# Attention scores of one token tile as three products of hi and lo parts instead of one float32 product, in a fused two-layer trunk

## The chip, the cores and the metric

The kernel runs on one core of a Trainium2 chip. The metric is device time in microseconds for one launch. The engines are called PE (TensorE, matrix products; its weight loads are listed as PEld), DVE (VectorE), ACT (ScalarE), POOL (GpSimd) and SP (SyncE, which here only issues DMA transfers). Each engine works through its own instructions in the order in which they were written for it.

## The reference, cut to what matters

Two layers, each a half-step SwiGLU feed-forward, a mixer and a second half-step feed-forward, with layer norms between. The input has 256 tokens of 1024 features in float32. The part of the mixer that the change touches:

```python
q = _rope(q.reshape(bsz, seq, N_DIFF_HEADS, 2, DIFF_HEAD_DIM), cos, sin)   # 8 heads, 2 maps of 64
k = _rope(k.reshape(bsz, seq, N_DIFF_HEADS, 2, DIFF_HEAD_DIM), cos, sin)
s = jnp.einsum('bqhmd,bkhmd->bhmqk', q_blk, k).astype(jnp.float32) * scale
s = jnp.where(mask, s, neg)                      # causal
p = jax.nn.softmax(s, axis=-1)
a = p[:, :, 0] - lam * p[:, :, 1]
return jnp.einsum('bhqk,bkhe->bqhe', a.astype(v.dtype), v)
```

## The kernel before, in words

The 256 tokens are two tiles of 128; t=0 is the first, t=1 the second. In causal attention the first tile's queries see 128 keys and the second tile's see 256.

**Weights and the split.** All weights are streamed once, 1 MB at a time, by the SP queue into a `raw` buffer (L153; 4 buffers). A float32 product is made of products in the faster float32r format: ACT writes a rounded copy `whi` (L166), DVE the remainder `wlo = raw - whi` (L168). There are 8 buffers for hi and 8 for lo parts. Activations are kept as hi and lo in the same way.

**The projections.** `gemm_a2` (L210 to L237) computes one 256-wide block of an input projection, features on partitions: per chunk eight products with `whi` on 512 columns (L220: the hi and lo parts of x side by side), later eight with `wlo` on 256 columns (L227). Then ACT evacuates half of the bank into `r` (L228, the instruction is kept as `emptied[0]`) and DVE adds the other half into `z` (L230 or L232, kept as `added[0]`). `gemm_b` and `rows_b` (L208) compute the other products with tokens on partitions. Products go to 4 "main" PSUM banks; scores, transposes and attention outputs to 4 "side" banks.

**The mixer.** After the values come four head pairs, hp0 to hp3 (L680 to L683). For each, `rope` (L563 to L581) projects and rotates q, then k: four small DMAs on the SP queue exchange the halves (L569), DVE multiplies by the cosine (L572), POOL by the sine (L573), DVE adds (L577). Then `attend` (L583 to L678) is set beside the stream of projections: scores (L597; the 64 features of one map lie on 64 partitions, so the two maps, m = 0 and 1, use two row groups), mask and maximum on DVE (L609), exp with sum on ACT (L611), the difference of the two maps (L620), transposes on PE (L634, L639), which ACT copies out as `aT` (L636 for t=1, 128x512; L641 for t=0, 128x256), the product with the values (L647, L649), RMS norm (L652 to L666, with POOL), transposes (L671) and the split result `hb` (L676, L677). After hp3 come the gates, whose projections end in `gz` (DVE) and L693 (ACT).

**Order.** PE's order is written by hand: a clock counts the weight of projections done (`beat`, 0.65 for a hi part and 0.35 for a lo part), and a generator that was set `beside` goes on when its delay has passed; `yield d` in it asks for the next turn d later. The order of DVE, ACT, POOL and SP is made by a scheduler that follows priorities; `behind(x)` asks for a place behind instruction x. What an engine finds at the head of its queue it waits for, whatever stands behind it.

**The filler.** After the last products, `idle` (L271 to L291) issues 52 products whose result nobody reads: 10 of 128x128, 16 of 64x256 and 16 of 64x128 on two row groups, 2 of 128x512 and 8 of 128x64, all in float32r, into two side banks.

Of the kernel before, what the change touches and what calls it, by code (L numbers as in the profile page):

```python
# [11 lines left out]
F32 = mybir.dt.float32  # L12
F32R = mybir.dt.float32r
BF16 = mybir.dt.bfloat16
I32 = mybir.dt.int32
AF = mybir.ActivationFunctionType
ALU = mybir.AluOpType
AX = mybir.AxisListType

P = 128  # L20
D = 1024
T = 256
# [7 lines left out]
HD = 64  # L30
# [20 lines left out]
def trunk(ctx, tc, x, xT, w13a, w13b, w2, wb, wqk, wa, wbr, wo, gateb, sgug, sgub, sguwT, sgubias, lam, diffg,  # L51
          lng, lnb, lngT, lnbT, cosT, sinT, out):
    nc = tc.nc
    V, A, G, PE = nc.vector, nc.scalar, nc.gpsimd, nc.tensor
# [15 lines left out]
    def name(s):  # L70
        serial[0] += 1
        return f"{s}_{serial[0]}"

    def bank():
        return psum.tile([P, 512], F32, tag="main", name=name("bank"))

    def side_bank():
        return psum.tile([P, 512], F32, tag="side", name=name("sbank"))

    def slots(s, n, dtype=F32):  # L80

        return [act.tile([P, 512], dtype, tag="slot", name=name(s)) for _ in range((n + 1) // 2)]
# [8 lines left out]
    def parts(f):  # L91
        return (lambda k: f(k)[:, :T]), (lambda k: f(k)[:, T:])
# [40 lines left out]
    def beside(task, delay):  # L133
        tasks.append([clock[0] + delay, task])
# [6 lines left out]
    latest, added, emptied, silu, turned_by = [None, None], [None], [None], [None], [None]  # L141

    def behind(ins):

        return tc.issue_after(ins) if ins is not None else nullcontext()

    def stream(src, width=CH, sub=HC, lent=(), after=(None, None)):

        step()
        raw = raw_pool.tile([P, CH], F32, tag="raw", name=name("raw"))
        nc.sync.dma_start(raw[:, :width], src)  # L153
        out = []
        for o in range(0, width, HC):
            if o // HC in lent:
                hi, lo = ([act.tile([P, 512], F32R, tag="slot", name=name(n)) for _ in range(2)] for n in ("lhi", "llo"))
                at = [(hi[j], lo[j]) for j in range(2)]
            else:
                hi = hi_pool.tile([P, HC], F32R, tag="hi", name=name("whi"))  # L160
                lo = lo_pool.tile([P, HC], F32R, tag="lo", name=name("wlo"))
                at = [(hi[:, p : p + sub], lo[:, p : p + sub]) for p in range(0, HC, sub)]
            for p, (h, w) in zip(range(0, HC, sub), at):
                r = raw[:, o + p : o + p + sub]
                with behind(latest[0]):
                    A.activation(h, r, AF.Copy)  # L166
                with behind(after[o // HC] or latest[1]):
                    V.tensor_tensor(out=w, in0=r, in1=h.bitcast(F32), op=ALU.subtract)  # L168
            out.append((hi, lo))
        return out  # L170
# [19 lines left out]
    def rsqrt4(v, scale):  # L190

        ve, y = sm("ve", 4), sm("yi", 4, I32)
        G.tensor_scalar(out=ve, in0=v, scalar1=scale, scalar2=None, op0=ALU.mult)
        G.tensor_scalar(out=y, in0=ve.bitcast(I32), scalar1=-0.5, scalar2=RSQRT_START, op0=ALU.mult, op1=ALU.add)
        y = y.bitcast(F32)
        for e in (-26 / 27, -8 / 9, -2 / 3):
            a, z = sm("nwa", 4), sm("nwy", 4)
            G.tensor_tensor(out=a, in0=y, in1=y, op=ALU.mult)
            G.tensor_tensor(out=a, in0=a, in1=ve, op=ALU.mult)
            G.tensor_scalar(out=a, in0=a, scalar1=3.0 * 2.0 ** e, scalar2=None, op0=ALU.subtract)  # L200
            G.tensor_tensor(out=z, in0=a, in1=y, op=ALU.mult)
            y = z
        return y
# [35 lines left out]
    def rows_b(ps, t, k0, piece, xh, xl, kts, c0=0, n=512):  # L239

        hi, lo = piece
        for j in range(2):
            k, o = k0 + j, j * 512 + c0
            wh, wl = (w[j][:, c0 : c0 + n] if isinstance(w, list) else w[:, o : o + n] for w in (hi, lo))
            three(ps[:, :n], xh(k)[:, t * P : (t + 1) * P], xl(k)[:, t * P : (t + 1) * P], wh, wl,
                  k == 0, k == kts - 1)
        beat(n / 1024)

    def gemm_b(src, kts, xh, xl, done, tail=4, last=()):

        blocks = [[(bank(), c, n) for c, n in (last if t else ()) or ((0, 512),)] for t in range(NT)]
        held = []
        for c in range(0, kts, 4):
            nk = min(4, kts - c)
            for i, piece in enumerate(stream(src[:, c * 512 : (c + nk) * 512], nk * 512)):
                k = c + 2 * i
                if k >= kts - tail:
                    held.append((k, piece))
                    continue
                for t in range(NT):  # L260
                    for ps, o, n in blocks[t]:
                        rows_b(ps, t, k, piece, xh, xl, kts, o, n)
        for t in range(NT):
            for ps, o, n in blocks[t]:
                for k, piece in held:
                    rows_b(ps, t, k, piece, xh, xl, kts, o, n)
                done(t, ps[:, :n], o, n)
        if last:
            idle(held, xh, xl)

    def idle(held, xh, xl):  # L271

        banks = [side_bank() for _ in range(2)]
        (k, (hi, lo)), (k1, (hi1, lo1)) = held[-2:]
        ws = [xh(k)[:, :P], xl(k)[:, :P], xh(k1)[:, :P], xl(k1)[:, :P]]
        ms = [hi[:, :512], lo[:, :512], hi1[:, :512], lo1[:, :512]]

        def one(i, n, m=None):
            r = slice(0, P) if m is None else slice(m * HD, (m + 1) * HD)
            PE.matmul(banks[m or 0][:, :n], ws[i % 4][r], ms[i % 4][r, :n], start=True, stop=True)  # L280

        for i in range(10):
            one(i, P)
        for n in (256, P):
            for i in range(8):
                for m in range(2):
                    one(i, n, m)
        for i in range(2):
            one(i, 512)
        for i in range(8):  # L290
            one(i, 64)  # L291

    def gemm_b2(srcs, xh, xl, done, norm=None):

# [207 lines left out]
    def ffn(l, f, i, norm, last=False):  # L502
# [26 lines left out]
        for j in range(FB, FT, 2):  # L529
            for m, z in gemm_a2([w13a[l, f, j - FB + m] for m in range(2)], both, lambda m: t512("silu")):  # L530
# [4 lines left out]
                if norm is None and j + m == FB:  # L535
                    beside(setup(s[:, :1]), 0)
        ln = Norm(l, i, 2.0 * ALPHA, 4.0 * EPS, s[:, :1], last)
        gemm_b(w2[l, f, 0], FT, hh, hl, lambda t, p, c, n: ln.part(t, 0, p))

        def done(t, p, c, n):  # L540
# [7 lines left out]
    def mixer(l, i, norm):  # L548
        xh, xl = parts(both)
# [33 lines left out]
        def attend(hp, qT, kT):  # L583
# [4 lines left out]
            def rows(z, m, j, o, n):  # L588
                return z[m * HD : (m + 1) * HD, j * T + o : j * T + o + n]

            def scores(t):

                nk = (t + 1) * P
                banks = [side_bank() for _ in range(2)]
                for j in range(2):
                    for m in range(2):
                        PE.matmul(banks[m][:, j * nk : (j + 1) * nk], rows(qT, m, j, t * P, P), rows(kT, m, j, 0, nk),  # L597
                                  start=True, stop=True)
                return banks

            def exps(t, banks):
                nk = (t + 1) * P
                pp = []
                for m in range(2):
                    o = m * 4 + t * 2
                    p = s512("pp", 4)[:, : 2 * nk]
                    for j in range(2):
                        s, a = slice(j * nk, (j + 1) * nk), slice(o + j, o + j + 1)
                        V.tensor_tensor_reduce(out=p[:, s], in0=banks[m][:, s], in1=mask[:, T - nk :], scale=-1.0,  # L609
                                               scalar=BIG, op0=ALU.add, op1=ALU.min, accum_out=mx[:, a])  # L610
                        A.activation(p[:, s], p[:, s], AF.Exp, bias=mx[:, a], scale=-1.0, accum_out=sums[:, a])  # L611
                    pp.append(p)
                return pp

            def less(t, pp):
# [5 lines left out]
                                            in1=pp[0][:, s], op0=ALU.mult, op1=ALU.add)  # L621
                return pp[0]

            banks = [scores(t) for t in (1, 0)]
            second, first = exps(1, banks[0]), exps(0, banks[1])
            V.reciprocal(out=rc, in_=sums[:, 4:])
# [34 lines left out]
            r = rsqrt4(ss, 1.0 / (2 * HD))  # L661
# [18 lines left out]
        for hp in range(HEADS // 2):  # L680
            qT = rope(wqk[l, hp, 0], HD ** -0.5)
            kT = rope(wqk[l, hp, 1], 1.0, hp == HEADS // 2 - 1)
            beside(attend(hp, qT, kT), 4.5)  # L683

        gates = []
        for br, sec in ((0, GA_), (1, GB_)):
# [17 lines left out]
        for t in range(NT):  # L704
            mv = sm("mv", 2)
            V.bn_aggr(out=mv, in_=vst[t])
            r = rsqrt(mv[:, 1:2], EPS)
# [66 lines left out]
    for l in range(DEPTH):  # L774
        norm = ffn(l, 0, 0, norm)
        norm = mixer(l, 1, norm)
        norm = ffn(l, 1, 2, norm, last=l == DEPTH - 1)
# [82 lines left out]
```

## Time and profile before

| what | value |
|---|---|
| median of 3 runs | 1241.08 us (1240.89 to 1241.84) |
| the profiled execution | 1241.04 us |
| its span, first to last instruction | 1239.3 us |
| granted TensorE clock | 1.000 |
| PE busy | 1234.4 us, 100% of the span |
| DVE busy | 874.2 us, 71% |
| ACT busy | 754.7 us, 61% |
| L597, the scores: records in both layers | 128 (64 of 64x256, 64 of 64x128) |

How to read it: a row of the timeline has the start in microseconds from the span's start, the duration, engine, line, operation, output <- input with the names of the program's tiles, shapes, count; in brackets how long the engine had been idle before and what ended that. Consecutive alike instructions are put together in one row (x16). A float32 product leaves two records, a float32r product one. The chain of waits follows the work that ended last back through what released it. In the groups by line the columns behind the count are busy time in all, mean nanoseconds of one, and idle time before.

### The profile page before, as it was taken

To read this page: it belongs to the slowest core of one execution; us is meant where nothing else is said; L and a number is where in the kernel's file an instruction comes from. 1 tells how busy PE (TensorE), PEld (TensorE's weight loads), DVE (VectorE), ACT (ScalarE), POOL (GpSimd) and SP (SyncE) were. 2 spreads that over 40 slices of the span, in tenths; PEclk is the share of its full clock that TensorE was granted. 3 is DMA by queue.
4 is the path that set the end of the run, shared out by engine and by line. 5 is a ranking of instruction groups with operands and counts; after the bars stand their busy time and mean duration, and the time that the engine had idled before them with its cause. 6 is when DMAs were issued, how large, how long until landed. Compare 5 with 4: busy or idle time off the path is not lost.

```text
span 1239.3 us, 17964 instructions
## 1 busy us (share of the span) xinstructions
PE 1234.4 (100%) x6747; PEld 1067.3 (86%) x6747; DVE 874.2 (71%) x1533; ACT 754.7 (61%) x1386; POOL 90.3 (7%) x182
## 2 busy tenths in 40 slices
PE   9999999999999999999999999999999999999998
PEld 8888888888888888888888888888888888888888
DVE  6766567886687977665676765678866879766753
ACT  6776446679665566664466664466885654766640
POOL 0100000244100000000000000003440000000000
PEclk9999999999999999999999999999999999999999
DMA  9765645654743745547545546556456456466540
GB/s 351 279 204 179 229 170 181 231 187 152 266 174 137 257 161 198 185 169 254 196 171 190 190 160 248 204 184 214 172 179 226 149 185 223 170 204 204 173 166 35
DMA packets 40681, 241.89 MB, mean 195 GB/s; under 512 B 5345, under 2 KB 6417, under 8 KB 14481
## 3 DMA queue, kind: packets, MB, share of 16 engines
q1 hardware_dynamic: 36624, 228.08, 52.5%
q0 software_dynamic: 3536, 12.13, 3.0%
q8 instruction: 53, 0.87, 0.3%
q10 hardware_dynamic: 432, 0.52, 0.1%
q14 instruction: 36, 0.29, 0.1%
HBM read 235.47 MB, written 1.05 MB: 191 GB/s over the span
## 4 chain that ended last, share of the span: by engine, by line
PE 97%; ACT 1%; DVE 1%; issue 0%; DMA 0%; SPq 0%; POOL 0%; DVEq 0%; POOLq 0%
PE bank L220 37%; PE bank L208 35%; PE bank L227 19%; PE bank L347 2%; PE sbank L597 1%; PE sbank L483 1%; PE sbank L730 1%; PE sbank L649 1%; ACT pp L611 0%; PE sbank L359 0%; PE sbank L517 0%; PE sbank L647 0%; PE sbank L671 0%; PE sbank L634 0%; DMA swap<-z 0%
## 5 line engine op out<-in xcount | busy, mean ns | idle before, releaser
L168 DVE TENSOR_TENSOR wlo<-raw,whi 128x1024 fp32r<-128x1024 f32 (+1 forms) x442 | 490.0, 1127 | 230.5 <-PE bank L227 127.2
L166 ACT ACTIVATE whi<-raw 128x1024 fp32r<-128x1024 f32 (+1 forms) x442 | 425.9, 978 | 286.5 <-PE bank L220 142.1
L220 PE MATMUL bank<-x,whi 128*128 128x512 f32 x1792 | 425.4, 391 | 0.0
L220 PEld LDWEIGHTS bank<-x,whi 128*128 128x128 f32 x1792 | 330.8, 188 | 66.2
L227 PE MATMUL bank<-x,wlo 128*128 128x256 f32 x1792 | 231.2, 284 | 0.0
L227 PEld LDWEIGHTS bank<-x,wlo 128*128 128x128 f32 x1792 | 225.2, 191 | 5.4
L208 PE MATMUL bank<-whi,hhi 128*128 128x512 f32 (+1 forms) x374 | 141.3, 378 | 0.0
L208 PE MATMUL bank<-wlo,hhi 128*128 128x512 f32 (+1 forms) x374 | 141.0, 377 | 0.0
L208 PE MATMUL bank<-whi,hlo 128*128 128x512 f32 (+1 forms) x374 | 140.9, 377 | 0.0
L228 ACT ACTIVATE r<-bank 128x256 f32<-128x256 f32 x256 | 96.8, 379 | 64.6 <-PE bank L227 64.1
L208 PE MATMUL bank<-whi,x 128*128 128x512 f32 x328 | 106.5, 394 | 0.0
L208 PEld LDWEIGHTS bank<-whi,hhi 128*128 128x128 f32 x374 | 70.4, 188 | 12.9
L208 PEld LDWEIGHTS bank<-whi,hlo 128*128 128x128 f32 x374 | 70.4, 188 | 12.9
L208 PEld LDWEIGHTS bank<-wlo,hhi 128*128 128x128 f32 x374 | 70.4, 188 | 12.7
L208 PEld LDWEIGHTS bank<-whi,x 128*128 128x128 f32 x328 | 61.6, 188 | 12.7
L208 PE MATMUL bank<-wlo,x 128*128 128x512 f32 x164 | 64.0, 390 | 0.0
L407 POOL DMA_DIRECT2D bc<-in_lng x6 | 3.2, 531 | 727.0 <-DVE bc L406 727.0
L489 ACT ACTIVATE xf<-sbank,ln_b,ln_g 128x128 f32<-128x128 f32 x80 | 30.0, 456 | 40.2 <-PE sbank L483 40.2
L230 DVE TENSOR_TENSOR silu<-bank,r 128x256 f32<-128x256 f32 x144 | 54.2, 418 | 0.2
L433 DVE SCALAR_TENSOR_TENSOR xtok<-xtok,bank 128x512 f32<-128x512 f32 (+1 forms) x25 | 16.6, 662 | 42.6 <-PE bank L208 42.6
L573 POOL TENSOR_TENSOR swap<-swap,sin_t 128x512 f32<-128x512 f32 x16 | 28.5, 1780 | 242.4 <-DMA swap<-z 141.9
L208 PE MATMUL bank<-lhi,x 128*128 128x512 f32 x120 | 39.8, 396 | 0.0
(178 smaller groups left out, 1262.1 us busy)
## 6 DMA issues: line engine op xcount, KB each, us to landing
raw<-in_w13a SPq DMA_DIRECT2D x72, 1024.0 KB, 5.0
raw<-in_w SPq DMA_DIRECT2D x40, 1024.0 KB, 4.9
raw<-in_wa SPq DMA_DIRECT2D x24, 1024.0 KB, 5.7
raw<-in_wb SPq DMA_DIRECT2D x16, 1024.0 KB, 4.9
raw<-in_wqk SPq DMA_DIRECT2D x16, 1024.0 KB, 5.1
raw<-in_wbr SPq DMA_DIRECT2D x16, 1024.0 KB, 5.0
raw<-in_w13b SPq DMA_DIRECT2D x12, 1024.0 KB, 5.0
raw<-in_wo SPq DMA_DIRECT2D x8, 1024.0 KB, 4.9
```

The costliest lines, as they stand in the source:

```text
L166: A.activation(h, r, AF.Copy)
L168: V.tensor_tensor(out=w, in0=r, in1=h.bitcast(F32), op=ALU.subtract)
L208: PE.matmul(ps, xx, w, start=start and n == 0, stop=stop and n == 2)
L220: PE.matmul(b[-1], hi[:, k * P : (k + 1) * P], xc(k), start=k == 0, stop=False)
L227: PE.matmul(b[n][:, :T], lo[:, k * P : (k + 1) * P], xc(k)[:, :T], start=False, stop=k == KT - 1)
L228: emptied[0] = A.activation(r[:, s], b[n][:, T:], AF.Copy, scale=scale).ins
L230: a = V.tensor_tensor(out=z[:, s], in0=b[n][:, :T], in1=r[:, s], op=ALU.add)
L347: PE.matmul(ps[t][m], x[:, j, o + t * P : o + (t + 1) * P], y, start=k0 + j == 0 and o == 0 and y is hi, stop=k0 + j == KT - 1 and y is lo)
L433: V.scalar_tensor_tensor(out=self.y[t][:, s], in0=self.y[t][:, s], scalar=self.scale, in1=ps, op0=ALU.mult, op1=ALU.add)
L483: PE.transpose(b[:, k * P : (k + 1) * P], self.y[t][:, h * 512 + k * P : h * 512 + (k + 1) * P], ident)
L489: A.activation(xf[:, s], b[:, s], AF.Identity, scale=self.gT[:, f], bias=self.bT[:, f])
L573: turned_by[0] = G.tensor_tensor(out=s3, in0=s3, in1=s, op=ALU.mult).ins
```

## The change

Three things are done.

1. `idle` and its call are removed.
2. The scores of t=1 become three products, q_hi k_hi + q_hi k_lo + q_lo k_hi, in float32r, accumulated in the same bank, on the same 64 partitions and two row groups. The scores of t=0 stay one float32 product. Per head pair, four float32 products of 256 columns become twelve of float32r.
3. For that, `attend` begins by making the parts: ACT copies k (128x512) and the second tile's q (128x256) into float32r, asked for behind `emptied[0]`; DVE subtracts these from k and q, asked for behind `added[0]`. Then it yields 2 before the scores. It is set beside the stream with a delay of 2.6 instead of 4.5, so that the scores' turn is due at 4.6. Three more activation slots per head pair are taken (27 in all are there).

```diff
-        if last:
-            idle(held, xh, xl)
-
-    def idle(held, xh, xl):
...
+                terms = ((q_hi, k_hi), (q_hi, k_lo), (q_lo, k_hi)) if t else ((qT, kT),)
                 for j in range(2):
-                    for m in range(2):
-                        PE.matmul(banks[m][:, j * nk : (j + 1) * nk], rows(qT, m, j, t * P, P), rows(kT, m, j, 0, nk),
-                                  start=True, stop=True)
+                    for n, (q, k) in enumerate(terms):
+                        for m in range(2):
+                            r = slice(m * HD, (m + 1) * HD)
+                            PE.matmul(banks[m][:, j * nk : (j + 1) * nk], q[r, j * P : (j + 1) * P] if t
+                                      else rows(q, m, j, 0, P), rows(k, m, j, 0, nk), start=n == 0,
+                                      stop=n == len(terms) - 1)
...
+            q2, k_hi, k_lo = (slots(n, 2, F32R)[0] for n in ("q2", "khi", "klo"))
+            q_hi, q_lo = q2[:, :T], q2[:, T:]
+            late = qT.rearrange("p (j t) -> p j t", j=2)[:, :, P:]
+            with behind(emptied[0]):
+                A.activation(k_hi, kT, AF.Copy)
+                A.activation(q_hi.rearrange("p (j t) -> p j t", j=2), late, AF.Copy)
+            with behind(added[0]):
+                V.tensor_tensor(out=k_lo, in0=kT, in1=k_hi.bitcast(F32), op=ALU.subtract)
+                V.tensor_tensor(out=q_lo.rearrange("p (j t) -> p j t", j=2), in0=late,
+                                in1=q_hi.bitcast(F32).rearrange("p (j t) -> p j t", j=2), op=ALU.subtract)
+            yield 2
...
-            beside(attend(hp, qT, kT), 4.5)
+            beside(attend(hp, qT, kT), 2.6)
```

More of the change, by code (lines that the diff above doesn't have):

```diff
@@ L267, in gemm_b @@
                 done(t, ps[:, :n], o, n)
-        if last:
-            idle(held, xh, xl)
-    def idle(held, xh, xl):
[L273 to L285, printed above, removed]
-                for m in range(2):
[L287 to L291, printed above, removed]
     def gemm_b2(srcs, xh, xl, done, norm=None):
@@ L594, in scores @@
                 banks = [side_bank() for _ in range(2)]
+                terms = ((q_hi, k_hi), (q_hi, k_lo), (q_lo, k_hi)) if t else ((qT, kT),)
                 for j in range(2):
-                    for m in range(2):
-                        PE.matmul(banks[m][:, j * nk : (j + 1) * nk], rows(qT, m, j, t * P, P), rows(kT, m, j, 0, nk),
-                                  start=True, stop=True)
+                    for n, (q, k) in enumerate(terms):
[4 more added lines that the diff above has]
+                                      stop=n == len(terms) - 1)
                 return banks
```

## The prediction

> **What bounds the kernel now.** I read the page's busy times first, then the chain that ended last, then the chain of waits around each stage that the change touches. Beside the 1239.3 us span, 1.74 us of the profiled execution's 1241.04 lie outside it; 1241.04 stands 0.04 under the median of the runs, 1241.08, so a sum on the one may be read on the other. About 0.2% (2.5 us) is what a measurement of this kernel can tell from no change.
>
> ```profile
> span 1239.3 us, 17964 instructions
> PE 1234.4 (100%) x6747; PEld 1067.3 (86%) x6747; DVE 874.2 (71%) x1533; ACT 754.7 (61%) x1386; POOL 90.3 (7%) x182
> PE 97%; ACT 1%; DVE 1%; issue 0%; DMA 0%; SPq 0%; POOL 0%; DVEq 0%; POOLq 0%
> ```
>
> PE is the bound: a removed PE nanosecond counts where PE isn't waiting, an added wait counts in full, and work on DVE or ACT costs only where PE comes to wait for it. Those averages hide the stages, so each of the eight attends (head pairs hp0 to hp3, two layers) is taken by itself.
>
> **The filler (idle, L280).** The chain of waits at the end:
>
> ```profile
> 1224.99 6.13 PE bank L208 x51
> 1235.78 0.40 DVE xtok L462
> ```
>
> The last real products end at 1231.12 on the chain, and from there to 1236.18 the chain is DVE's normalisation, behind which only the output's transfer is left. The 52 filler matmuls stand beside it, nothing waits for them, and DVE's end does not move: **0**. The filler runs on an engine that nothing needs any more, so neither a gain nor a loss has a path inside this program. What PE's missing activity might do to an execution that follows, no row shows; I take nothing for it.
>
> **The products on PE.** Timeline of PE around hp0's scores (the third row from a narrow window), L597's table by window (in its second pair of columns PE's busy time and the records), and two pieces of layer 0's chain, eight products behind hp2's scores and eight elsewhere:
>
> ```profile
> 236.42 1.58 PE L597 MATMUL sbank<-qk,qk 64*128 64x256 f32 x16
> 237.93 0.73 PE L220 MATMUL bank<-x,whi 128*128 128x512 f32 x2
> 236.74 0.60 PE L597 MATMUL sbank<-qk,qk 64*128 64x256 f32 x4
> 236.40:237.38 0.98, 0.96 (x8) 0.88 (x10) 1.00 0.88 326
> 266.35 2.04 PE bank L220 x8
> 271.63 1.84 PE bank L220 x8
> ```
>
> Sixteen records take 236.42 to 237.93. Up to 237.38 eight have begun, all of t=1: 0.96 us for the four f32 products of 256 columns (two records each, a pair for the two row groups); the second pair begins at 236.74, so the first took 0.32 and the other three (0.96 - 0.32) / 3 = 0.215. The other eight, t=0, take 0.55. Eight L220 behind scores take 2.04 instead of 1.84: 0.2 for coming back from 64 rows. That return, and the entry, occur once before and after the change. The nearest price for the new products is the filler's own 64-row part, alternating over two row groups in fp32r:
>
> ```profile
> 1232.11 0.38 PE L280 MATMUL sbank<-whi,hhi 64*128 64x256 f32 x2
> 1232.33 0.28 PE L280 MATMUL sbank<-wlo,hlo 64*128 64x256 f32 x2
> 1233.16 0.23 PE L280 MATMUL sbank<-whi,hhi 64*128 64x128 f32 x2
> ```
>
> First pair 0.22 (1232.11 to .33), then seven pairs to 1233.16: 0.83 / 7 = 0.118 a pair. Twelve products are six pairs: 0.22 + 5 x 0.118 = 0.81, against 0.96: **-0.15 per attend**, -1.2 for eight, if PE waits for nothing. A switch from fp32r to f32 inside 64 rows, which t=0 now needs, no row shows; 0 to 0.2 by the entry and return above. I take 0, as the entry that the 0.22 holds is paid once anyway, and keep +0.2 x 8 for the range.
>
> A page speaks against this: the Trainium skill, "TensorE: Matmul & The Clock Gate", section "Part 3: Packing small matmuls", says that a weight load overlaps running matmuls only when the row groups differ. By it, the next pair of products, in rows that are still running, would wait for its weights, and a pair would cost about a load and a matmul, twice the filler's. The filler's 0.118 a pair, all in two row groups in turn, disagrees; the rival is priced from rows below.
>
> **The split on ACT and DVE.** Per attend ACT gets a 128x512 and a 128x256 copy, DVE a 128x512 and a 128x256 subtraction. Groups by form, 229 to 285 us:
>
> ```profile
> L636 ACT ACTIVATE aT<-sbank 128x512 f32<-128x512 f32 x3 | 1.8, 598 | 0.1
> L641 ACT ACTIVATE aT<-sbank 128x256 f32<-128x256 f32 x3 | 1.2, 388 | 0.0
> L577 DVE TENSOR_TENSOR qk<-qk,swap 128x512 f32<-128x512 f32 x7 | 4.8, 685 | 2.3 <-POOL swap L573 2.3
> L230 DVE TENSOR_TENSOR z<-bank,r 128x256 f32<-128x256 f32 x6 | 2.4, 420 | 0.0
> ```
>
> An instruction follows about 0.1 us before the end of the one ahead (at hp1 below, 247.03 + 0.60 against 247.53), so I take 0.50 + 0.28 = 0.78 us of ACT and 0.60 + 0.33 = 0.93 of DVE. Whether PE sees them is a matter of order, and both kernels' built instruction order (no times in it) is known, engine by engine. PE's order is otherwise unchanged. What it puts before the scores:
>
> *hp0.* khi and qhi run behind the second whi, ahead of the evacuation r; klo and qlo behind a wlo.
>
> ```profile
> 234.69 0.38 ACT L228 ACTIVATE r<-bank 128x256 f32<-128x256 f32 x1 [0.58 <-PE bank L227]
> 235.60 1.66 DVE L168 TENSOR_TENSOR wlo<-raw,whi 128x1024 fp32r<-128x1024 f32 x1
> ```
>
> ACT stands idle there; DVE's new 0.93 runs before the 235.60 row, done by about 236.0, 0.4 ahead of the scores. **-0.15** in each layer; without that cover up to +0.4. What is pushed back is the wlo of a later product, for which 8 lo buffers stand.
>
> *hp1, where the order turns.* Before, ACT does r, aT1, aT0, r, whi. After: r, khi, qhi, r, whi, aT1, aT0. ACT is in order, and that whi must wait until PE has read its buffer for the last time (8 hi buffers). Timelines of ACT and PE before:
>
> ```profile
> 247.03 0.60 ACT L636 ACTIVATE aT<-sbank 128x512 f32<-128x512 f32 x1
> 247.53 0.38 ACT L641 ACTIVATE aT<-sbank 128x256 f32<-128x256 f32 x1
> 250.03 1.06 ACT L166 ACTIVATE whi<-raw 128x1024 fp32r<-128x1024 f32 x1 [1.45 <-PE bank L220]
> 248.00 2.00 PE L220 MATMUL bank<-x,whi 128*128 128x512 f32 x8
> 249.93 1.58 PE L597 MATMUL sbank<-qk,qk 64*128 64x256 f32 x16
> 251.44 1.43 PE L220 MATMUL bank<-x,whi 128*128 128x512 f32 x5
> ```
>
> The whi waits for the eight L220 just ahead of the scores (248.00 to 250.00). There are four side banks; t=0's two are those that aT1 and aT0 read. So t=0 now waits: whi 250.03, aT1 from 250.98 (0.95 a whi) to 251.58, aT0 from 251.48 to 251.86. PE is done with t=1 at 249.93 + 0.81 = 250.74, starts t=0's first bank at 251.6, the second at 251.9, and the next L220 at 251.9 + 0.54 = 252.44, against 251.44: **+1.0**. The PV products at 254.3 need aT later than that. Layer 1 has the same order and rows:
>
> ```profile
> 862.66 1.06 ACT L166 ACTIVATE whi<-raw 128x1024 fp32r<-128x1024 f32 x1 [1.45 <-PE bank L220]
> 862.55 1.58 PE L597 MATMUL sbank<-qk,qk 64*128 64x256 f32 x16
> ```
>
> whi 0.11 behind the scores' start, as in layer 0 (0.10): **+1.0** again. A klo late by up to 0.8 here would be hidden under this wait. Queued behind the waiting whi: aT and then the exps, which wait for the scores anyway.
>
> *hp2.* Both r's, khi and qhi stand before aT, ahead of whi.
>
> ```profile
> 262.79 0.39 ACT L641 ACTIVATE aT<-sbank 128x256 f32<-128x256 f32 x1
> 264.77 1.58 PE L597 MATMUL sbank<-qk,qk 64*128 64x256 f32 x16
> ```
>
> aT ended at 263.18; 0.78 more, and an r of 0.3 put before it, gives 264.3, needed at 265.6; but what hp1 left behind on ACT and DVE may take it. Between -0.15 and +0.3; I take **0**.
>
> *hp3, layer 0.* Here ACT has no gaps (timeline of ACT; chain for PE):
>
> ```profile
> 278.78 0.46 ACT L676 ACTIVATE hb<-sbank,dgs 128x256 fp32r<-128x256 f32 x1
> 279.88 0.39 ACT L641 ACTIVATE aT<-sbank 128x256 f32<-128x256 f32 x1
> 280.16 1.51 PE sbank L597 x16
> ```
>
> khi, q behind hb (279.14): done 279.99; klo behind it and a wlo to 280.6, qlo to 280.9; aT at 281.05. Needed, from 280.16: klo 280.5, qlo 280.75, aT 281.0. Without lag 0.2 late, less 0.15: +0.1. With hp2's 0.78 + 0.93 still behind: +1.0. ACT's gaps before 269 us absorb most of that, so **+0.3**.
>
> *hp3, layer 1.* PE already waits, and the chain of waits runs through ACT, DVE, POOL and a swap from 868.5 on:
>
> ```profile
> 868.50 1.35 ACT pp L611 x7
> 892.34 0.46 ACT L676 ACTIVATE hb<-sbank,dgs 128x256 fp32r<-128x256 f32 x1
> 892.71 0.70 PE L597 MATMUL sbank<-qk,qk 64*128 64x256 f32 x2
> 893.61 1.57 PE L597 MATMUL sbank<-qk,qk 64*128 64x256 f32 x14 [0.20 <-ACT aT L636]
> 895.11 0.73 PE L220 MATMUL bank<-x,whi 128*128 128x512 f32 x2
> ```
>
> khi and q behind hb end at 893.54, klo 894.0, qlo 894.35, t=1 by 894.6, aT0 by 894.7 to 895.0, next L220 at 895.25 to 895.6: +0.15 to +0.5 without lag; up to +1.7 with hp2's 1.7 us on that chain. I take **+0.7**.
>
> **Queues.** On SP two moves a layer: a raw load of 1 MB goes ahead of hp1's first swap, hp2's last swap ahead of a raw. POOL's order stays.
>
> ```profile
> 240.08 1.29 POOL L573 TENSOR_TENSOR swap<-swap,sin_t 128x512 f32<-128x512 f32 x1 [3.91 <-DVE mx L609]
> 244.56 0.68 DVE L577 TENSOR_TENSOR qk<-qk,swap 128x512 f32<-128x512 f32 x1
> ```
>
> The swap was multiplied by 241.37 and added at 244.56: 3.2 us of slack against about half a raw's time (5.0, page's part 6); 0, and up to +2 for a layer if it landed past that. The swap moved forward can only land earlier.
>
> **Sum.** hp0 2 x -0.15 = -0.3; hp1 2 x +1.0 = +2.0; hp2 0; hp3 0.3 + 0.7 = +1.0; filler 0: **+2.7 us, 1243.7** (1241.04 + 2.7).
>
> **Rivals.** (1) *Lag dominates.* ACT and DVE, short by 0.78 and 0.93 per attend, don't catch up: hp2 +0.3 each, hp3 +1.0 and +1.7, so -0.3 + 2.0 + 0.6 + 2.7 = +5.0, 1246.0. For it: ACT without gaps from 277 on, no slack in layer 1; against it: PE's own wait at hp1 gives both engines 1.0 us. (2) *The other side, not slower:* hp1's aT is not late. It decides whether whi behind PE's last L220 really gates: it does as soon as that L220 ends after 248.9 or so (1.1 us before 250.0). If the buffer came free earlier, t=0 would start in time, the saving of 0.15 x 8 would stay: 1239.8, faster by 0.1%. Against: the 1.45 us of ACT idle, ascribed to L220 in both layers. (3) *Weight loads aren't hidden:* pairs in fp32r would go as the f32 pairs do, 0.215 a pair: 0.22 + 5 x 0.215 = 1.30, +0.34 instead of -0.15 for six attends not covered by hp1's wait: +2.9 more, 1246.6. Against: 0.118 in the filler. (4) *hp1 alone:* hp2 and hp3 cost nothing beyond their saving; 2.0 - 6 x 0.15 = +1.1, 1242.1. That the change doesn't do what it says is out: the built order holds twelve fp32r products per attend.
>
> **How the numbers follow.** Forecast 0.50 (own range 1242.6 to 1244.9; a bit over half of it beyond 1243.56); rival 1 0.18; rival 2 0.11; rival 3 0.07; rival 4 0.14. Slower by over 0.2%: 0.29 + 0.18 + 0.07 = 0.54; the same: 0.21 + 0.14 + most of rival 2, 0.41; faster 0.05. The range leaves out rival 2 and rival 3: 1241.2 to 1246.2.
>
> **What would show it.** In the profile after: t=1's L597 at 0.118 a pair, t=1 in 0.8; at hp1 of both layers an ACT order whi, aT, aT and PE idle of 0.8 to 1.2 us ahead of t=0, put down to ACT aT; hp0 without wait; hp3 with waits on khi, klo or qlo. L280 gone and the DVE tail unchanged. Wrong it would be with no PE wait at hp1 (rival 2), pairs at 0.2 (rival 3), or PE idle of over 1 us at hp3 in both layers (rival 1).

## The result, and the profile after

| | before | after |
|---|---|---|
| median | 1240.95 us (6 runs, 1240.40 to 1241.84) | 1245.35 us (6 runs, 1245.19 to 1245.83) |
| ratio | | 1.0034, 95% interval 1.0023 to 1.0044 |
| span of the profiled execution | 1239.3 us | 1243.6 us |

The change costs 4.4 us, 0.34%. The forecast was +2.7, 1243.7; its full range, 1241.2 to 1246.2, holds 1245.35, its own narrower one, 1242.6 to 1244.9, does not. The page of after, the rows that answer to those of before (span; busy; chain by engine):

```profile
span 1243.6 us, 17969 instructions
PE 1233.0 (99%) x6727; PEld 1063.5 (86%) x6727; DVE 887.8 (71%) x1549; ACT 759.1 (61%) x1402; POOL 89.7 (7%) x182
PE 92%; DVE 4%; ACT 1%; POOL 1%; issue 1%; DMA 0%; SPq 0%; DVEq 0%; ACTq 0%; POOLq 0%
```

PE is still busy nearly all the time, but 5 points of the chain, some 60 us, have moved from it to DVE, POOL and what lies between them. (A share of the chain says what released what, not what was lost.) The scores stand now on L576, the splits on L608, L609 (ACT: khi, q) and L611, L612 (DVE: klo, q), mask and exp on L589 and L591, aT on L627 and L632, the transposes of `on` on L662, the swap's DMA on L545 and POOL's multiply on L549.

**Where the time came from.** PE's order is the same in both but for the scores, so the start of the first product behind each place can be set side by side (the difference is after minus before, of the same product; the step is what one place adds to the difference).

| place | layer 0: before, after (difference) | step | layer 1: before, after (difference) | step | forecast of the step |
|---|---|---|---|---|---|
| scores of hp0 begin | 236.42, 235.89 (-0.53) | | 849.05, 851.21 (+2.17) | | |
| behind hp0's scores | 237.93, 237.70 (-0.22) | +0.3 | 850.55, 853.02 (+2.47) | +0.3 | -0.15, -0.15 |
| behind hp1's scores | 251.44, 252.33 (+0.90) | +1.1 | 864.06, 867.67 (+3.61) | +1.1 | +1.0, +1.0 |
| behind hp2's scores | 266.27, 266.99 (+0.71) | -0.2 | 878.90, 882.38 (+3.48) | -0.1 | 0, 0 |
| behind the transposes of hp0's `on` | 273.67, 275.00 (+1.34) | **+0.6** | 886.29, 890.54 (+4.25) | **+0.8** | none |
| behind hp3's scores | 281.60, 283.82 (+2.22) | +0.9 | 895.11, 899.35 (+4.24) | 0 | +0.3, +0.7 |

Layer 0 adds 2.75, layer 1 2.07; the -0.53 ahead of them arises in the first 7 us, where the kernels differ in nothing, and varies from run to run (-0.9 to +0.2 in the kernels below). 2.75 + 2.07 - 0.53 is the 4.3 us between the spans.

Two steps at hp3 need care, since the kernel before waits there too, in some executions. In layer 1 its scores and what keeps them waiting take 2.40 us (892.71 to 895.11), and those of after as long (896.95 to 899.35): the step of 0 is one wait in place of another. In layer 0 they take 1.51 in before's trace, but 2.24 in the trace of experiment 1, which has no split, a step of +0.73. The traces of 3, 4, 5 and 9 have +0.8 to +1.3 at that place, so some of it is likely the split's; how much of the +0.9 is, one trace of after doesn't tell.

The price of the products was right. Timeline of PE in after at hp2, where nothing is waited for:

```profile
265.64 0.38 PE L576 MATMUL sbank<-khi,q 64*128 64x256 f32 x2
265.86 0.28 PE L576 MATMUL sbank<-klo,q 64*128 64x256 f32 x2
...
266.45 0.61 PE L576 MATMUL sbank<-qk,qk 64*128 64x128 f32 x8
266.99 1.89 PE L220 MATMUL bank<-x,whi 128*128 128x512 f32 x7
```

t=1 takes 0.81 (265.64 to 266.45), first pair 0.22, and t=0 0.54: the switch to float32 costs nothing. hp0 was to look the same, and doesn't:

```profile
235.89 0.39 PE L576 MATMUL sbank<-khi,q 64*128 64x256 f32 x2
236.25 0.38 PE L576 MATMUL sbank<-klo,q 64*128 64x256 f32 x2
236.59 0.50 PE L576 MATMUL sbank<-khi,q 64*128 64x256 f32 x4
```

The second pair begins 0.36 behind the first instead of 0.22, the third 0.34 behind the second instead of 0.12. These are the products that need klo, then q_lo. DVE and POOL at that place, then all klo by the lines' view (the row's three figures are minimum, median and maximum in ns):

```profile
234.41 1.79 DVE L611 TENSOR_TENSOR klo<-qk,khi 128x512 fp32r<-128x512 f32 x1
236.12 0.41 DVE L612 TENSOR_TENSOR q<-qk,q 128x256 fp32r<-128x256 f32 x1
```

```profile
233.67 1.98 POOL L549 TENSOR_TENSOR swap<-swap,sin_t 128x512 f32<-128x512 f32 x1 [3.60 <-DMA swap<-z]
```

```profile
L611 DVE TENSOR_TENSOR klo<-qk,khi x8: 678/684/1786, 234.4 to 897.1; 128x512 fp32r<-128x512 f32 x8
```

klo takes 0.68 elsewhere and 1.79 here (1.78 at hp0 of layer 1): POOL's multiply ends at 235.65, and klo 0.55 later. The Trainium skill, "SBUF — State Buffer", section "SBUF: two separate sides", says that an operation of DVE with two SBUF inputs and one of POOL lock a shared port pair for a whole instruction, and that the later one stands still meanwhile. The rows agree: klo behaves as if it ran behind POOL's multiply.

hp1 looks as forecast (ACT, then PE):

```profile
249.82 1.06 ACT L166 ACTIVATE whi<-raw 128x1024 fp32r<-128x1024 f32 x1 [1.44 <-PE bank L220]
250.79 0.58 ACT L627 ACTIVATE aT<-sbank 128x512 f32<-128x512 f32 x1
251.27 0.38 ACT L632 ACTIVATE aT<-sbank 128x256 f32<-128x256 f32 x1
```

```profile
249.72 0.38 PE L576 MATMUL sbank<-khi,q 64*128 64x256 f32 x2
...
251.42 0.98 PE L576 MATMUL sbank<-qk,qk 64*128 64x128 f32 x8 [0.17 <-ACT aT L627]
252.33 0.50 PE L220 MATMUL bank<-x,whi 128*128 128x512 f32 x1
```

whi waits for PE, aT stands behind it, t=0 begins at 251.42. But the chain of waits of after does not go through this wait. It leaves PE at 233 us and comes back at 274.6:

```profile
251.13 1.95 DVE wlo L168
253.07 0.60 DVE qk L553
253.68 0.60 DVE qk L548
254.28 0.33 DVE pp L589
254.66 1.98 ACT pp L591 x8
...
261.00 0.34 DVE z L232
...
263.21 2.05 DMA swap<-z
...
265.42 1.28 POOL swap L549
266.70 1.15 POOL ss L651
...
273.59 1.00 ACT on L657 x3
274.63 0.62 PE sbank L662 x3
```

From hp1's split on DVE over the exps of hp1 to the z of the next rope, its swap, POOL's multiply, the RMS norm of hp0 behind that multiply in POOL's queue, and so to the transposes of `on`. Its wlo took 1.95, beside a multiply of POOL, and `ss` 1.15 instead of 0.2, beside a wlo. DVE is what has no room there. Busy time in 254 to 269 us (after, then before; the columns behind the length are PE, PEld, DVE, ACT, POOL; the time for which DVE stands still beside POOL counts as busy):

```profile
254.00:269.00 15.00, 15.00 (x105) 13.21 (x104) 14.69 (x38) 11.99 (x38) 4.69 (x5) 1.00 0.54 178
```

```profile
254.00:269.00 15.00, 15.00 (x102) 13.20 (x101) 12.99 (x41) 11.82 (x39) 6.29 (x12) 1.00 0.55 185
```

What PE itself shows at the two later places, the transposes of hp0's `on` and hp3's scores, both in layer 0:

```profile
274.63 0.62 PE L662 MATMUL sbank<-ident,on 128*128 128x128 f32 x3 [0.26 <-ACT on L657]
...
281.43 0.69 PE L576 MATMUL sbank<-khi,q 64*128 64x256 f32 x2
282.27 0.38 PE L576 MATMUL sbank<-klo,q 64*128 64x256 f32 x2 [0.15 <-DVE klo L611]
```

So two readings stood against each other. **Order**: the wait for aT at hp1 is a loss of 1.1 us a layer by itself, as predicted, and the rest comes on top. **Lag**: DVE (with POOL and ACT behind it) is too slow from hp0 to hp3, PE waits for that lag wherever it shows first, and a wait taken away at one place comes back at the next.

### The profile page after: what moved, and what is told of

Read it like the earlier page. It is cut to its first block, busy times and chain, and to the rows that moved or that the text cites. A ratio compares the mean times of both kernels' runs of the same rounds, so it can differ in the third digit from the quotient of the medians.

```text
span 1243.6 us, 17969 instructions
## 1 busy us (share of the span) xinstructions
PE 1233.0 (99%) x6727; PEld 1063.5 (86%) x6727; DVE 887.8 (71%) x1549; ACT 759.1 (61%) x1402; POOL 89.7 (7%) x182
## 3 DMA queue, kind: packets, MB, share of 16 engines
HBM read 235.47 MB, written 1.05 MB: 190 GB/s over the span
## 4 chain that ended last, share of the span: by engine, by line
PE 92%; DVE 4%; ACT 1%; POOL 1%; issue 1%; DMA 0%; SPq 0%; DVEq 0%; ACTq 0%; POOLq 0%
PE bank L208 35%; PE bank L220 34%; PE bank L227 18%; PE bank L323 2%; ACT pp L591 1%; DVE wlo L168 1%; PE sbank L459 1%; PE sbank L721 1%; DVE pp L600 0%; DVE qk L553 0%; DVE qk L548 0%; PE sbank L335 0%; PE sbank L662 0%; PE sbank L640 0%; PE sbank L493 0%
## 5 line engine op out<-in xcount | busy, mean ns | idle before, releaser
L549 POOL TENSOR_TENSOR swap<-swap,sin_t 128x512 f32<-128x512 f32 x16 | 24.8, 1548 | 245.4 <-DMA swap<-z 222.7
```

Source lines behind the costliest of these rows:

```text
L549: turned_by[0] = G.tensor_tensor(out=s3, in0=s3, in1=s, op=ALU.mult).ins
```

## The experiments

Each was timed in five rounds against the kernel before on the same chip; before was 1241.03 in the first group (1 to 4), 1241.34 in the second (5 to 8) and 1241.12 in the third (9 to 12).

**1. The filler alone.** Before without `idle`:

```diff
-        if last:
-            idle(held, xh, xl)
```

> The kernel before without the filler products, nothing else. If the filler costs and gives nothing, as forecast: within 0.5 us of the kernel before (1240.95), PE's last real product and the DVE tail at the same places. Rival, in which the filler was worth something (a loss of its removal is a part of the +4.4): 1 to 4 us slower.

1241.25 us, ratio 1.0002 (0.9993 to 1.0011). The filler is worth nothing that a measurement to about 1 us can show, as forecast.

**2. The products alone.** Before without the filler, and

```diff
+                terms = ((both(2)[:, :T], both(0)), (both(2)[:, :T], both(1)), (both(2)[:, T:], both(0))) if t else ((qT, kT),)
```

> Before without the filler, its t=1 scores as twelve float32r products, but made from parts of x that are there anyway: no copy, no subtraction, scores timed as in before (the scores of the second tile are not those of q and k). If the price of the products on PE is 0.118 us a pair: t=1 in 0.81 us instead of 0.96, eight times -0.15, about 1239.7. Rival, the products or the change of type to float32 behind them cost more than they save: 1241 or more, and t=1 plus t=0 longer than 1.51 us.

1239.44 us, ratio 0.9988 (0.9979 to 0.9997). Timeline of PE at hp0:

```profile
236.00 0.97 PE L576 MATMUL sbank<-x 64*128 64x256 f32 x12
236.81 0.61 PE L576 MATMUL sbank<-qk,qk 64*128 64x128 f32 x8
237.35 0.96 PE L220 MATMUL bank<-x,whi 128*128 128x512 f32 x3
```

0.81 and 0.54. The saving that the change is after exists: 1.6 us measured (0.4 to 2.6 by the interval). The trace holds 0.15 at hp0 to hp2 of both layers, 0.9 in all, and not the full 1.2: at hp3 the scores take 1.73 and 2.57 us instead of 1.35, in layer 1 with a wait of 0.84 for aT. All of the loss, 4.4 + 1.6 = 6.0 us, is the split and what it moves.

**3. The split alone.** After, with its t=1 scores in float32 again; copies and subtractions are made and not read:

```diff
-                terms = ((q_hi, k_hi), (q_hi, k_lo), (q_lo, k_hi)) if t else ((qT, kT),)
+                terms = ((qT, kT),)
```

> After, with the copies and subtractions made but the t=1 scores again one float32 product that doesn't read them. If the loss is carried by what DVE and ACT do later because of the split (orders and lag), it stays: hp1's wait for aT is there, and the time is 1244.3 to 1245.2. Rival, the loss is the products' own waits for klo and qlo: they are gone, 1241.5 to 1243.

1246.13 us, ratio 1.0040 (1.0027 to 1.0054). More than expected, and no less than after (the two intervals overlap): without any product that waits for klo or q_lo, the loss is all there. PE steps by 0 at hp0 in this kernel (the wait for klo is gone), but by +1.1 at hp1 in both layers and +1.3 at hp3 of layer 0. The products' own waits aren't the loss.

**4. The order at hp1 alone.** After, with one constraint in each layer, on the whi that stood ahead of aT (the 84th and 287th of the stream); nothing else moves:

```diff
-                with behind(latest[0]):
+                with behind(AFTER_AT.get(whi_n[0]) and aT_ins[AFTER_AT[whi_n[0]]] or latest[0]):
                     A.activation(h, r, AF.Copy)
```

> After with one order constraint in each layer: at hp1 ACT's whi behind both aT copies instead of ahead; no other instruction of any engine moves. If the wait for aT at hp1 is itself the loss, as in the prediction: PE's step at hp1 falls from +1.1 to at most +0.45 in each layer, and the time by 1.4 to 2.2 us, to 1243.2 to 1244.0. Rival, read off the chain of waits of after, which runs from 233 to 274 us through DVE, ACT, the swap's transfer and POOL and not through PE's wait: the wait only moves, to the transposes of on (L662), which then wait 0.7 us longer each; 1244.9 to 1245.4.

1245.28 us, ratio 1.0036 (1.0023 to 1.0048): nothing gained, though PE's step at hp1 fell as expected, to +0.42 in both layers, what is left being the products' wait for klo. ACT, then PE, then who kept PE waiting (total us, times, longest):

```profile
248.24 0.59 ACT L631 ACTIVATE aT<-sbank 128x512 f32<-128x512 f32 x1
```

```profile
251.05 0.61 PE L580 MATMUL sbank<-qk,qk 64*128 64x128 f32 x8
251.59 2.11 PE L224 MATMUL bank<-x,whi 128*128 128x512 f32 x8
...
254.98 0.49 PE L642 MATMUL sbank<-val,aT 128*128 128x128 f32 x2 [0.34 <-DVE mx L593]
```

```profile
PE sbank L642 <- DVE mx L593: 1.1, 2, 0.8
```

aT is done 2.6 us earlier (248.24 instead of 250.79), t=0 follows t=1 without a gap, and 0.74 us is gained at 251.59 against 252.33. It is given back 3.4 us later: the product with the values needs a side bank, of which there are four, and the mask of the scores (L593) hasn't read it yet. (The rival had put that wait at the transposes; they step by +0.7 and +0.8, much as in after.) DVE is late there for its own reasons. This decides against **order** as the cause by itself.

**5 and 6. One half of the split at a time.**

```diff
-            with behind(added[0]):
-                V.tensor_tensor(out=k_lo, in0=kT, in1=k_hi.bitcast(F32), op=ALU.subtract)
...
+                terms = ((q_hi, k_hi), (q_hi, k_hi), (q_hi, k_hi)) if t else ((qT, kT),)
```

> After without the two DVE subtractions: the three products all read the rounded parts (so the lo parts are left out of the scores of the second tile); ACT's two copies and the PE work stay, and ACT's order at hp1 is aT before whi again. If the loss is DVE's added 0.93 us per head pair: hp0, hp1, hp2 each gain about 0.15, the transposes of on don't wait, and only hp3 may still wait for ACT: 1239.6 to 1241.2. Rival, ACT's copies carry the loss: 1242.5 or more.

1242.58 us, ratio 1.0010 (1.0001 to 1.0019). A miss by 1.4 us: about half of the loss is gone. hp0 and hp1 don't wait, but the transposes of `on` still step by +0.6 in both layers, where none was expected, and hp3 of layer 0 by +0.95, with q behind hb on ACT (timeline of PE):

```profile
280.87 1.05 PE L576 MATMUL sbank<-khi,q 64*128 64x256 f32 x12 [0.71 <-ACT q L609]
```

And the other half:

```diff
-            with behind(emptied[0]):
-                A.activation(k_hi, kT, AF.Copy)
...
+                V.tensor_tensor(out=k_lo, in0=kT, in1=kT, op=ALU.subtract)
```

> After without ACT's two copies: DVE makes its two subtractions in the same sizes from q and k alone, the products read parts of x for the rounded parts (the scores of the second tile are not those of q and k). ACT's order at hp1 is aT before whi. If DVE's added work is the loss: it stays, with hp1 now waiting for the exps or for klo in place of aT, 1243.5 to 1245.3. Rival, ACT's work or its order: 1239.7 to 1242.

1244.57 us, ratio 1.0026 (1.0016 to 1.0035). With DVE's part alone the loss stays, though ACT's order at hp1 is that of before and t=0 waits for no aT. PE waits at the transposes of `on` instead:

```profile
PE sbank L659 <- ACT on L654: 2.2, 4, 0.8
```

Against the products alone, each run taken from its own group's before, ACT's part costs 2.8 us, DVE's 4.8, both 6.0: the two don't add up. That the same stretch waits for whichever comes last is the likely reason; it is not shown by itself. (The scheduler moves other instructions too when a half is missing, so these are not pure prices.) DVE's part costs its 4.8 although no klo of experiment 6 takes over 0.69 us.

One figure of the traces speaks for **lag** directly. From the first score of hp0 to the first product behind the transposes of hp0's `on` in layer 0, PE takes 39.1 us in after, where it waits at hp1 for aT, 39.1 in experiment 4, where it waits there for klo alone, and 39.3 in experiment 6, where it doesn't wait there (37.25 in before, 37.7 in experiment 5 without DVE's part). The waits ahead of it don't move that instant; DVE's part does.

**7 and 8. POOL's hand in it.** After, and before without the filler as its control, with

```diff
-            turned_by[0] = G.tensor_tensor(out=s3, in0=s3, in1=s, op=ALU.mult).ins
+            turned_by[0] = G.tensor_tensor(out=s3[:, :, :32], in0=s3[:, :, :32], in1=s[:, :, :32], op=ALU.mult).ins
```

> After with POOL's multiply by the sine cut to 64 of 512 columns (the rest of the rotation's sine part is left out). In after klo takes 1.79 us at hp0, beside POOL's multiply, and 0.68 elsewhere. If DVE is slowed by POOL working beside it, klo at hp0 falls to about 0.7, hp0 gains 0.15 instead of losing 0.3, DVE's chain is about 1 us shorter per rope and the transposes of on no longer wait: 1240.0 to 1242.5. Rival, klo is long at hp0 for another reason (its input, a queue): klo stays near 1.8 and the time at 1244.5 or more.

> Control for the shortened POOL multiply: the kernel before without the filler, with the same cut. PE didn't wait for that chain in before but for 0.6 to 0.9 us at hp3 of layer 1: 1240.0 to 1241.2 by both theories. If it fell as far as after does, the cut would say nothing on the change.

After falls to 1240.89, ratio 0.9997 (0.9989 to 1.0006); the control to 1240.14, ratio 0.9991 (0.9982 to 1.0000). The cut is worth 4.5 to 5 us to after and about 1 to before. klo by the lines' view, then what PE waits for:

```profile
L611 DVE TENSOR_TENSOR klo<-qk,khi x8: 679/684/814, 234.9 to 892.9; 128x512 fp32r<-128x512 f32 x8
```

```profile
PE sbank L576 <- ACT aT L627: 1.5, 2, 0.7
```

No klo is over 0.81 us: POOL working beside DVE was what made it long. hp0 steps by -0.15, the transposes by 0 and hp3 of layer 0 by -0.16, as the products without a wait would; hp3 of layer 1 steps by -1.05, since before's own wait there is gone (-0.89 in the control); only hp1's wait for aT is left, with its +1.1 a layer.

**9. Both gates at once.** The cut of 7 and the order of 4 together:

> After with POOL's multiply cut to 64 of 512 columns and, besides, ACT's whi behind aT at hp1 (the most of the rotation's sine part is left out). The cut alone gave 1240.89, the order alone 1245.28. If hp1 has two gates of about the same height, ACT's order and DVE's lag, then with the lag gone the order is worth its full 1.1 to 1.3 us in each layer: 1238.3 to 1239.2. Rival, the order never mattered: 1240.5 to 1241.3.

1241.08 us, ratio 1.0001 (0.9993 to 1.0010). A miss: with hp1's wait gone (step -0.14 there) nothing is gained again. The wait reappears at the transposes of `on` (+0.3 and +0.5) and at hp3: +0.8 in layer 0, and in layer 1 a step of -0.07 where 7 had -1.05. PE at hp3 of layer 0, and the chain of waits that leads there:

```profile
280.86 0.39 PE L580 MATMUL sbank<-klo,q 64*128 64x256 f32 x2 [0.16 <-DVE klo L615]
```

```profile
264.61 2.47 POOL ss L655
...
272.24 1.28 ACT on L661 x4
...
277.61 0.96 ACT whi L170
278.59 1.22 DVE wlo L172
...
280.13 0.69 DVE klo L615
```

So even this shorter chain isn't in time once PE no longer stands still for 1.1 us at hp1. (It isn't free of POOL and DVE meeting either: its `ss` takes 2.47 us, beside three DVE instructions in a row.) The wait at hp1 had given DVE, POOL and ACT that time. My reading of experiment 7, that the lag was gone and aT alone was left, fell with this run.

**10 to 12. The multiply by the sine on DVE**, a version that leaves nothing out: in after with the order of 4, in after alone, and in before.

```diff
-            turned_by[0] = G.tensor_tensor(out=s3, in0=s3, in1=s, op=ALU.mult).ins
...
+                    V.tensor_tensor(out=s3, in0=s3, in1=s, op=ALU.mult)
                     V.tensor_tensor(out=r, in0=r, in1=sw, op=ALU.add)
...
-            with behind(turned_by[0]):
+            with nullcontext():
```

> After with ACT's whi behind aT at hp1, and the whole multiply by the sine on DVE just ahead of the add, nothing left out. DVE gets 0.6 us more per rope, but is no longer slowed beside POOL by about 1.1, and the 1.3 to 2.0 us of POOL leave the chain. If that slowing is what the split's DVE work met: 1238.3 to 1240.3, faster than both kernels. Rival, DVE is simply full: 1242 or more.

> After with the sine's multiply on DVE, without the order constraint for aT. If hp1's order costs 1.1 to 1.3 us a layer once DVE is in time: 2.2 to 2.6 us more than with the constraint, provided the scheduler leaves whi ahead of aT. Rival: the same time as with it.

> Control: the kernel before with the sine's multiply on DVE. PE waited there only for 0.6 to 0.9 us at hp3 of layer 1: 1240.0 to 1241.3. If it is as fast as the changed kernel with both edits, the three products gain nothing even there.

1241.58 (ratio 1.0003, 0.9994 to 1.0012), 1241.21 (1.0000, 0.9991 to 1.0009) and 1239.98 (0.9992, 0.9983 to 1.0000). The eleventh tells nothing on the order, since its scheduler put aT ahead of whi by itself, and the two are the same. The tenth is a miss: 1238.3 to 1240.3 was expected, faster than both kernels. Sixteen multiplies more on DVE, 0.68 us each by its rows, make after about 4 us faster: POOL's multiply, by its lock on DVE and its place in the chain, cost more than the work does. (With it, POOL's `ss` no longer queues behind that multiply.) But neither of the two is faster than before, and in before the same edit gives about 1 us, because hp3 of layer 1 no longer waits there: with the multiply on DVE, the changed kernel is still 1.2 to 1.6 us slower than the unchanged one. No scores wait in the tenth, all eight take 1.35 us; PE waits at the transposes of `on`, a step of +1.40 in each layer, behind POOL's RMS norm. Two rows of POOL there:

```profile
261.62 2.34 POOL L655 TENSOR_TENSOR ss<-s,ss 128x4 f32<-128x4 f32 x1 [128.63 <-ACT sbank L652]
264.65 2.92 POOL L202 TENSOR_TENSOR nwa<-yi 128x4 f32<-128x4 f32 x1
```

The shortest of such instructions take 0.20 us; here DVE is at work beside them without a break. Moving the multiply frees DVE of POOL, but not POOL of DVE. The twelfth is the fastest of all that leave nothing out, at the edge of what can be told from no change.

## Why the prediction was right and wrong

The direction and the full range were right, and in part by luck: the size was 4.4 instead of 2.7 us, outside the forecast's own narrower range, and the wait that made up most of the sum was not the cause.

- **Filler 0**: right, to about 1 us (experiment 1).
- **Products -0.15, switch to float32 0**: right (2, and hp2's rows). The rival with weight loads not hidden is out: 0.118 a pair.
- **hp0, -0.15**: wrong, +0.3. The step that failed is klo's price, 0.60. DVE's 0.68 became 1.79 beside POOL's multiply. This stood in the trace of before: the 1.66 us wlo that the prediction quotes as its cover takes 1.23 elsewhere, and overlaps that same multiply.
- **hp1, +1.0**: right in its place, its order, its instant and its size (+1.1 in both layers), and yet not a loss of its own: taking it away gains nothing (4 and 9). The step that failed is the sum, in which the 2 x 1.0 stood as if every place's waits added. Behind hp1, DVE's chain delivers later than PE needs it, with or without that wait.
- **hp2, 0**: -0.2 and -0.1; aT and klo were in time there. Its scores take 1.35 us also in 4, 6 and 9, where PE was held up less at hp1 or not at all, so the wait at hp1 isn't needed for that.
- **The transposes of `on`**: the term that is missing, +0.6 and +0.8. The prediction followed the split to the scores, and not the delay on through z, the swap's transfer and POOL's queue to the next wait of PE. It is DVE's in the main, but ACT's copies alone bring +0.6 there too, with PE earlier (5).
- **hp3, +0.3 and +0.7**: +0.9 and 0. In layer 0 klo, behind a wlo and `hb` on DVE, was the bounded "up to +1.0", as far as experiment 1 lets one trace tell; in layer 1 a wait for klo took the place of before's wait for aT, at the same length.
- **Queues**: no step of PE could be put down to SP's moves.

What took place is the first rival, that the lag of ACT and DVE dominates (+5.0 by its working, 4.8 by the table's steps), in part at other places than it named. The sign that the prediction gave for it, PE idle for over 1 us at hp3 in both layers, came, if only just: the scores there take 2.39 and 2.40 us, and 1.35 without a wait. Its argument against itself, that PE's wait at hp1 gives both engines 1 us, is what experiment 9 shows.

What stays open: how the loss divides between DVE's own 0.93 us per head pair and the lock with POOL, in either direction. Cutting POOL short also takes its multiply out of the chain, and moving the sine to DVE does both at once; no run held POOL's time and freed only the port. That klo itself is slow at hp0 is not the main part: in experiment 6 it isn't.

## What to carry to other kernels

Where a slow engine feeds a fast one over several places, the waits at those places are not terms of a sum: ask of each wait what would be late next if it went, and take the slowest chain over the whole stretch, here DVE's from hp0 to hp3. In this case a correctly found wait was worth nothing, since the chain of waits, read over more than one place, did not pass through it. And a duration of DVE is only to be used with what POOL does at that time: the same subtraction was 0.68 and 1.79 us.

## What the runs showed of the hardware that was not expected

- A 128x512 subtraction on DVE that began 0.74 us after a POOL multiply of 1.98 us took 1.79 us instead of 0.68, and ended 0.55 us after POOL; with that multiply cut to an eighth, the longest of the eight took 0.81.
- It works both ways: POOL's 128x4 `ss` took 1.15 us on the chain of after, beside a wlo, and 2.47 in experiment 9, where the median of before's eight is 0.24 (0.71 at most). In experiment 10 a 128x4 instruction of POOL stood for 2.92 us, beside four DVE instructions without a gap between them, so its wait was not limited to one of them.
- A float32 product on 64 rows right behind float32r products on the same rows began 0.12 us after the last of them (hp2: 266.33 to 266.45), no later than one more float32r pair would have.
